# RWKV backward direction reversed in time, its triangles transposed through DRAM, one output accumulator per direction, and preparation handed out by VectorE time

## The chip, the cores and the metric

The kernel runs on one core of a Trainium2 chip, as one launch. The metric is the device time of that launch in microseconds (us). Five engines work beside each other from queues of their own: TensorE (PE in the profile, its weight loads PEld), VectorE (DVE), ScalarE (ACT), GpSimd (POOL) and SyncE (SP), which here issues every DMA. An engine takes its instructions in program order; waits between engines go over semaphores.

## The reference, cut to what matters

One layer of a hybrid block over 512 tokens `x` (width 1024) with 256 context tokens `ctx`: an RWKV-7 mixer, a convolution and an mLSTM side by side, a gated merge, and an MLP, all in float32. The change concerns the RWKV mixer. It has 8 heads of width 64, and its scan is run twice, forward and backward in time, from the state that the same direction left on the context:

```python
def _rwkv7_scan(s0, w, k, v, kk, a, r, reverse, emit):
    ...
    def step(S, inp):
        w_t, k_t, v_t, kk_t, a_t = inp[:5]
        S = (S * w_t[:, :, None, :]
             - jnp.einsum('bhvk,bhk->bhv', S, kk_t)[..., None] * (kk_t * a_t)[:, :, None, :]
             + v_t[..., None] * k_t[:, :, None, :])
        y = jnp.einsum('bhvk,bhk->bhv', S, inp[5]) if emit else None
        return S, y
    S, y = lax.scan(step, s0, xs, reverse=reverse)
    return S, (jnp.moveaxis(y, 0, 1) if emit else None)
...
    for d in range(2):
        rev = d == 1
        s_ctx, yc = _rwkv7_scan(s0, w_c, k_c, fc[2], fc[3], a_c, fc[0], rev, emit_ctx)
        _, yl = _rwkv7_scan(s_ctx, w_l, k_l, fl[2], fl[3], a_l, fl[0], rev, True)
        y_lat = y_lat + yl
```

## The kernel before, in words

Every dense product is three fp32r matmuls over high and low halves of its operands (the weight `raw` is split by ScalarE at L159 and by GpSimd at L160). The 768 tokens are 12 chunks of 64 (`NCH`, `CH`): 0 to 7 are latent, 8 to 11 context. The two directions `d` of a head lie on the two halves of the partitions, `HF[0]` and `HF[1]`. Two heads make a pair `j`, and there are four pairs.

The operands and values of all pairs are made early, in `operands` (a scan over the decays per direction at L386 and L387, products, spills `sp_al` and `sp_bk`) and `values` (`sp_v`). The backward direction has the tokens in the same order as the forward one, so its chunks are visited by the second list of `ORDER`, its masks are upper where the forward ones are lower (`gmf`, `gmb`), and its scan has negative strides.

Class `Rwkv` then has two parts. The **preparation** of a pair (`ctx`, `lat`, `gram`, `transposed`, `invert`) loads the spilled operands, multiplies them chunk by chunk into `pg` (L1006), masks these into `LT`, `LR` and `AL` (L1009, L1011, L1017), and inverts the 64x64 unit triangles in `LT`. For that it cuts each triangle into two 32x32 diagonal blocks, brings them with four VectorE transposes into `N` (L1045; one partition for each of the matrices), runs 30 elimination steps of two instructions each (`tmp` L1050, `N` L1052), transposes the result into `TN` (L1055, L1057) and back into `LT` (L1075, four), and makes the off-diagonal block with small matmuls `px` and `py` (L1066 to L1083). The **chain** runs over the 12 chunks of a pair, one after the other, in three hops a chunk: `ch` (L1133), its negation `xc` on ScalarE (L1137), `ch` (L1139), the copy `UV` (L1142), `ch` (L1148) and the new state `SV` on VectorE (L1149). A chunk of the chain is called a round here; two `SV` instructions, one per direction, end it.

`weave(j)` writes the program of chain `j`: after each of its 36 hops come `PACE[p]` steps of the preparation of pair `j+1` (so many `yield`s of it), then dense matmuls `dg` of the gates and projections (`DENSE`). The output of the pair (`output`, `py`) is accumulated for both directions in one PSUM tile, and `tail(j-1)` normalises it in the next weave. Weave 3 has loads of the modulation weights `wad` in place of a preparation. The preparation of pair 0 runs ahead of the weaves, among the last parts of the mLSTM. The names `x<-y` in the rows are an instruction's written and read tiles.

```python
PACE = [4] * 8 + [3] * 8 + [2] * 12 + [0] * 8
...
            for _ in range(PACE[p] if j < 3 else self.MODS):
                self.paced(last, step(nxt))
```

## Time and profile before

| | |
|---|---|
| three runs | 1365.77, 1371.26, 1374.08 us (median 1371.26) |
| the profiled execution: its time, its span | 1368.34 us, 1366.6 us |
| busy over the span: PE, DVE, ACT, POOL | 1238.3 (91%), 858.2 (63%), 511.2 (37%), 583.0 (43%) us |
| granted TensorE clock, mean | 0.955 of full speed |
| share of the chain of waits: PE, DVE, DMA | 42%, 17%, 6% |
| operands and values | from 131 to 291 us |
| mLSTM fronts and convolution; the mLSTM's end and preparation 0 | 291 to 434; 434 to 531 us |
| weaves 0, 1, 2 | 531 to 793 us |
| weave 3; merge and MLP | 793 to 934; 934 to 1366 us |

The shares are means over stages with different limits. The stages were cut where the first instructions of a part begin; a stage's busy times and its own chain of waits tell what bounds it.

### The profile page before, as it was taken

The numbers are of one execution on the slowest core, as the hardware profiler recorded it, in microseconds if no ns is written. First come the engines' busy times: TensorE is split into PE (matmuls) and PEld (weight loads), VectorE is DVE, ScalarE is ACT, GpSimd is POOL, SyncE is SP. The second block draws the span as 40 slices with busy tenths as digits, with TensorE's granted clock in tenths as the row PEclk, the third lists the DMA queues.
The fourth block names the chain that finished last, engine by engine and source line by source line (L and its number), as shares of the span: only waits on it lengthen the run. The fifth ranks groups of instructions, "written<-read, shape, count | busy, mean of one in ns | idle before, by whom it ended". The sixth has DMA issues, their size and how long they took to land.

```text
span 1366.6 us, 21733 instructions
## 1 busy us (share of the span) xinstructions
PE 1238.3 (91%) x8020; PEld 964.7 (71%) x8020; DVE 858.2 (63%) x1513; ACT 511.2 (37%) x1048; POOL 583.0 (43%) x547
## 2 busy tenths in 40 slices
...
GB/s 375 99 58 63 197 264 245 229 75 70 200 78 91 125 53 150 85 131 60 136 117 48 86 164 146 275 247 234 139 131 142 136 93 93 154 101 95 129 98 87
DMA packets 101457, 187.85 MB, mean 137 GB/s; under 512 B 10708, under 2 KB 29396, under 8 KB 100328
## 3 DMA queue, kind: packets, MB, share of 16 engines
...
HBM read 148.64 MB, written 29.40 MB: 130 GB/s over the span
## 4 chain that ended last, share of the span: by engine, by line
PE 42%; DVE 17%; DMA 6%; issue 2%; ACT 1%; POOL 0%; SPq 0%; DVEq 0%; ACTq 0%; POOLq 0%
PE pt L1301 16%; PE pd L1370 13%; DMA wad<-wada 5%; PE dg L545 4%; DVE N L1052 3%; DVE tmp L1050 3%; PE pg L1006 2%; DVE N L1045 2%; DVE accm L641 1%; PE pd L715 1%; DVE LT L1075 1%; PE ch L1133 1%; DVE SV L1149 1%; PE dl L293 1%; PE ch L1139 1%
## 5 line engine op out<-in xcount | busy, mean ns | idle before, releaser
L160 POOL TENSOR_TENSOR wlo<-raw,whi 128x512 fp32r<-128x512 f32 x296 | 430.8, 1461 | 554.8 <-ACT whi L159 496.3
L159 ACT CAST whi<-raw 128x512 fp32r<-128x512 f32 x296 | 181.7, 619 | 322.0 <-PE pt L1301 114.1
L293 PE MATMUL dl<-hh,whi 128*128 128x512 f32 (+1 forms) x344 | 143.2, 416 | 5.2 <-ACT kT L791 4.3
L293 PE MATMUL dl<-hh,wlo 128*128 128x512 f32 (+1 forms) x344 | 140.5, 408 | 0.0
L293 PE MATMUL dl<-hl,whi 128*128 128x512 f32 (+1 forms) x344 | 139.7, 406 | 0.0
L1370 PE MATMUL pd<-h2h,wlo 128*128 128x512 f32 (+1 forms) x272 | 105.2, 388 | 0.0
L1370 PE MATMUL pd<-h2l,whi 128*128 128x512 f32 (+1 forms) x272 | 104.5, 386 | 0.6 <-POOL h2l L1353 0.6
L1396 DVE TENSOR_TENSOR x<-pt,modb 128x512 f32<-128x512 f32 x8 | 5.5, 691 | 154.8 <-PE pt L1301 154.8
L1370 PE MATMUL pd<-h2h,whi 128*128 128x512 f32 (+1 forms) x272 | 102.3, 383 | 0.2 <-ACT h2h L1350 0.2
L1301 PE MATMUL pt<-whi,h1l 128*128 128x512 f32 x256 | 99.7, 389 | 0.0
L1301 PE MATMUL pt<-whi,h1h 128*128 128x512 f32 x256 | 99.7, 389 | 0.0
L1301 PE MATMUL pt<-wlo,h1h 128*128 128x512 f32 x256 | 99.2, 389 | 0.0
L293 PEld LDWEIGHTS dl<-hh,whi 128*128 128x128 f32 (+1 forms) x344 | 66.9, 194 | 20.4 <-ACT kT L791 4.5
L1374 DVE TENSOR_TENSOR relu<-relu 128x512 f32<-128x512 f32 x32 | 43.7, 1367 | 57.9 <-ACT relu L1373 57.8
L641 DVE SCALAR_TENSOR_TENSOR accm<-wad,scz,accm 128x512 f32<-128x512 f32 x56 | 57.6, 1028 | 34.2 <-DMA wad<-wada 33.6
L293 PEld LDWEIGHTS dl<-hh,wlo 128*128 128x128 f32 (+1 forms) x344 | 66.8, 194 | 14.3 <-issue 0.4
L293 PEld LDWEIGHTS dl<-hl,whi 128*128 128x128 f32 (+1 forms) x344 | 66.6, 194 | 13.8 <-issue 1.3
L1146 POOL TENSOR_TENSOR sps<-SV,PL 64x128 f32<-64x128 f32 x88 | 40.0, 454 | 78.6 <-DVE SV L1149 75.5
L545 PE MATMUL dg<-hl,whi 128*128 128x512 f32 x144 | 65.8, 457 | 0.0
L545 PE MATMUL dg<-hh,whi 128*128 128x512 f32 x144 | 65.0, 451 | 0.0
L545 PE MATMUL dg<-hh,wlo 128*128 128x512 f32 x144 | 64.9, 450 | 0.0
L1370 PEld LDWEIGHTS pd<-h2l,whi 128*128 128x128 f32 x272 | 51.7, 190 | 12.5 <-POOL h2l L1353 0.9
...
## 6 DMA issues: line engine op xcount, KB each, us to landing
...
sp_al<-al SPq DMA_DIRECT2D x8, 640.0 KB, 5.2
```

The lines of the kernel that those rows point to most:

```text
L159: A.copy(hi[:, :], raw[:, :])
L160: G.tensor_tensor(lo[:, :], raw[:, :], hi[:, :], ALU.subtract)
L293: PE.matmul(ps_[0:M, :], lhsT=w[:, ko:ko + M], rhs=x[seg][:, k, :], start=(n == 0), stop=(n == 3 * KT - 1))
L545: yield lambda w=w, x=x, k=k, ko=ko, n=n: PE.matmul(ps[:, :], lhsT=w[:, ko:ko + P], rhs=x[:, k, :], start=(n == 0), stop=(n == 3 * KT - 1))
L641: V.scalar_tensor_tensor(o, t[:, :], sc[:, k, 0:1], o, ALU.mult, ALU.add)
L1006: PE.matmul(ps[hf, i, :, :], lhsT=BK[dd, c, x, :], rhs=al[:, c] if lat else AL[d][dd, 8 + c:9 + c, :], start=True, stop=True)
L1050: V.tensor_tensor(tv, N[:, s + 1:32, s:s + 1].to_broadcast([P, n, s]), N[:, s:s + 1, 0:s].to_broadcast([P, n, s]), ALU.mult)
L1052: V.tensor_tensor(N[:, s + 1:32, 0:s], N[:, s + 1:32, 0:s], tv, ALU.add)
L1146: last["Pool"] = G.tensor_tensor(sps[hf], SV[d][hf, c, :, :], PL[hf, c, :].unsqueeze(2).to_broadcast([64, 2, CH]), ALU.mult)
L1301: PE.matmul(pss[i][:, :], lhsT=x[:, k, ts_], rhs=w[:, :], start=(k == 0 and n == 0), stop=(k == nk - 1 and n == 2))
L1370: PE.matmul(ps[:, ts_], lhsT=w[:, ko:ko + P], rhs=x[:, k, ts_], start=(k == 0 and n == 0), stop=(k == 7 and n == 2))
L1374: V.tensor_tensor(t[:, :], t[:, :], t[:, :], ALU.mult)
```

## The change

The backward half of every operand is turned round in time before it is used: `kr`, `rr` and `vr` are copies by GpSimd with reversed strides, `wdt` and `adt` are written reversed, and the values exist twice in DRAM (`sp_v`, `sp_vr`). Both directions then share one chunk order, one scan of 128 partitions, and masks of one form (`gmo` for a direction's own half of the product, `gmx` for the other). The masks of a chunk group become one instruction of 128 partitions, which writes `LT` and what was `LR`, and two for `AL`.

```diff
-            SY.dma_start(BK[HF[d]], kb[HF[h]])
-            SY.dma_start(rj[HF[d], :], r[HF[h], :])
+            SY.dma_start(BK[HF[d]], kb[d][HF[h]])
+            SY.dma_start(rj[HF[d], :], r[d][HF[h], :])
...
-        V.tensor_tensor_scan(ctf[0:64, :], mkf[0:64], cw[0:64, :], 0.0, ALU.mult, ALU.add)
-        V.tensor_tensor_scan(ctf[64:128, ::-1], mkf[64:128, ::-1], cw[64:128, ::-1], 0.0, ALU.mult, ALU.add)
+        V.tensor_tensor_scan(ctf, mkf, cw[:, :], 0.0, ALU.mult, ALU.add)
...
-        SY.dma_start(sp["bk", hd][:, :], BK.rearrange("p c x t -> p (c x t)"))
+        SY.dma_start(sp["bk", hd][HF[0], :], BK[HF[0]].rearrange("p c x t -> p (c x t)"))
+        for x in range(2):
+            SY.dma_start(sp["bk", hd][HF[1], :].rearrange("p (c x t) -> p c x t", x=2, t=CH)[:, :, 1 - x, :], BK[HF[1], :, x, :])
...
+        vr = S1.tile([P, NCH, 2, CH], F32, tag="kr", name="vr").rearrange("p c x t -> p (c x t)")
+        for a, z in SEG:
+            G.tensor_copy(vr[:, a:z], vj[:, a:z][:, ::-1])
+        for nm, vx in (("v", vj), ("vr", vr)):
+            for c2 in range(2):
+                pt = PS1.tile([P, 3, P], F32, tag="tp", name="tp", bufs=1)
+                for i in range(3):
+                    PE.transpose(pt[:, i, :], vx[:, (c2 * 3 + i) * P:(c2 * 3 + i + 1) * P], ident)
+                vt = S1.tile([P, 3, P], F32, tag="vt", name="vt", bufs=2)
+                A.copy(vt[:, :, :], pt[:, :, :])
+                SY.dma_start(sp[nm, j][c2 * 384:c2 * 384 + 384, :].rearrange("(c t) v -> t c v", t=P), vt[:, :, :])
...
+        kr = S1.tile([P, NCH, 2, CH], F32, tag="kr", name="kr")
+        rr = S1.tile([P, NT], F32, tag="rr", name="rr")
+        for c in (slice(0, 8), slice(8, 12)):
+            G.tensor_copy(kr[:, c], kbs[j][:, c][:, ::-1, :, ::-1])
+        G.tensor_copy(rr[:, :], rj[:, ::-1])
         for h in range(2):
-            operands(j, h, kbs[j], rj)
+            operands(j, h, (kbs[j], kr), (rj, rr))
```

The blocks for the inversion go through DRAM: `LT` is written to `sp_lt` and read back as `N`; after the steps `N` is written to `sp_n` and read back into `LT` in runs of 32 floats. The `TN` transposes become one.

```diff
+        for h, c4 in ((0, 2), (1, 2), (0, 0), (0, 1), (1, 0), (1, 1)):
+            lat = c4 < 2
+            cost = 0.7 if lat else 0.43
+            own = products(h, c4, 0)
+            if masked:
+                other(*masked, 1)
+            yield cost
+            g = h * 12 + c4 * 4
+            dst = LT[:, ::-1, g:g + 4, :] if lat else LT[:, 0:1, g:g + 4, :]
+            V.tensor_tensor(dst.rearrange("p x c t -> p c x t"), own[:, :, :, :], mask("gmo", 2 if lat else 1), ALU.mult)
+            oth = products(h, c4, 1)
+            if c4 == 1:
+                hs = slice(h * 12, h * 12 + 12)
+                SY.dma_start(lt[:, h * 12 * CH:(h + 1) * 12 * CH], LT[:, 0, hs, :].rearrange("p g t -> p (g t)"))
+                for q in range(4):
+                    o, qs = 32 * (q % 2), slice(32 * q, 32 * q + 32)
+                    SY.dma_start(self.N[32 * q + h * 12:32 * q + h * 12 + 12],
+                                 lt[qs, h * 12 * CH:(h + 1) * 12 * CH].rearrange("s (g t) -> g s t", t=CH)[:, :, o:o + 32])
+            yield cost
+            other(h, c4, oth, 0)
+            masked = h, c4, oth
+            yield cost
+        other(*masked, 1)
+        yield cost
...
+        for h in range(2):
+            yield from self.transposed(j, h, (2, 0, 1))
+        if after:
+            after()
+        for s in range(30, 0, -1):
+            n = 31 - s
+            tv = tmp[:, 0:n * s].rearrange("p (t j) -> p t j", t=s)
+            V.tensor_tensor(tv, N[:, 0:s, s:s + 1].to_broadcast([P, s, n]),
+                            N[:, s:s + 1, s + 1:32].to_broadcast([P, s, n]), ALU.mult)
+            V.tensor_tensor(N[:, 0:s, s + 1:32], N[:, 0:s, s + 1:32], tv, ALU.add)
+            yield 0.24 + n * s / 450
+        G.memset(N.rearrange("p a b -> p (a b)")[:, 0:1024:33], 1.0)
+        SY.dma_start(n_[:, :], N.rearrange("p a b -> p (a b)"))
         for q in range(4):
-            d, bl = q // 2, q % 2
-            qs = slice(32 * q, 32 * q + 32)
-            src = LT[qs, :, 32 * bl:32 * bl + 32].rearrange("p g t -> p t g")
-            V.transpose(N[qs] if d == 0 else N[qs].rearrange("p a b -> p b a"), src)
-            yield
-        for s in range(1, 31):
-            n = 31 - s
...
-        G.memset(N.rearrange("p a b -> p (a b)")[:, 0:1024:33], 1.0)
-        V.transpose(TN[0:32].rearrange("p g s -> p s g"), N[0:32].rearrange("p t s -> p s t"))
-        yield
-        V.transpose(TN[96:128].rearrange("p g s -> p s g"), N[96:128])
-        yield
-        xs, ps = [], []
+            o, qs = 32 * (q % 2), slice(32 * q, 32 * q + 32)
+            SY.dma_start(LT[qs, :, o:o + 32], n_[32 * q:32 * q + 24, :].rearrange("g (s t) -> s g t", t=32))
+        V.transpose(TN.rearrange("p g s -> p s g"), N[:, :, :])
...
-        for q in range(4):
-            d, bl = q // 2, q % 2
-            qs = slice(32 * q, 32 * q + 32)
-            src = N[qs] if d == 0 else N[qs].rearrange("p a b -> p b a")
-            V.transpose(LT[qs, :, 32 * bl:32 * bl + 32].rearrange("p g t -> p t g"), src)
```

The chain's `UU` copies go, since `UV` now keeps each direction on its own half; the output gets one PSUM tile per direction, which the tail adds; each step of the preparation yields its VectorE time, and a hop takes steps until 1.3 us are given out; loads are moved.

```diff
-PACE = [4] * 8 + [3] * 8 + [2] * 12 + [0] * 8
+PACE = 1.3
...
+            for d, nm in enumerate(("v", "vr")):
+                src = self.sp[nm, j][c4 * 4 * CH:(c4 + 1) * 4 * CH, :].rearrange("(c t) v -> t c v", t=CH)
+                for dst in (SV[d], UV[d]):
+                    SY.dma_start(dst[HF[1 - d], cs].rearrange("p c h v -> p c (h v)"), src)
...
-        py = self.py = self.PSC.tile([P, NT], F32, tag="o", name="py")
...
+        py = self.py = [self.PSC.tile([P, NT], F32, tag=("o", "ob")[d], name="py") for d in range(2)]
...
-                o = py[HF[h], c * CH:(c + 1) * CH]
                 for d in range(2):
-                    PE.matmul(o, lhsT=self.SV[d][:, c, h, :], rhs=self.AL[d][sl[h]][:, c, :], start=(d == 0), stop=False)
-                PE.matmul(o, lhsT=self.UU[:, c, h, :], rhs=self.LR[sl[h]][:, c, :], start=False, stop=True)
+                    o = py[d][HF[h], c * CH:(c + 1) * CH]
+                    PE.matmul(o, lhsT=SV[d][:, c, h, :], rhs=self.AL[d][sl[h]][:, c, :], start=True, stop=False)
+                    PE.matmul(o, lhsT=UV[d][HF[d], c, h, :], rhs=LR[HF[d], h * 12 + c, :], start=False, stop=True)
...
-            for d, c, ch, hf in zip(range(2), cs, chs, HF):
-                if c < 8:
-                    last["ACT"] = A.copy(self.UU[hf, c, :, :], ch[HF[0], 1])
...
+        def spend():
+            nonlocal budget, over
+            c = next(nxt, None)
+            over = c is None
+            budget -= c or 0
...
-            for _ in range(PACE[p] if j < 3 else self.MODS):
+            if j < 3:
+                budget += PACE
+                while budget > 0 and not over:
+                    self.paced(last, spend)
...
+            if p == 30 and j < 3:
+                self.load(j + 1, (0,))
...
-            self.load(j + 1, (0, 1))
+            self.load(j + 1, (1,))
+        if j < 2:
+            self.fetch(j + 2, "lat")
...
-        A.copy(y[:, :], self.py[:, :])
+        A.copy(y[:, :], self.py[0][:, :])
+        V.tensor_tensor(y[:, :], y[:, :], self.py[1][:, ::-1], ALU.add)
```

Three places of the program's order. On VectorE, the second round of weave 1: from one pair of `SV` to the next, before (its first two rows, then the masks of half a chunk group each; the next `SV` stand behind the cut):

```order
L1149 TENSOR_TENSOR SV_4802<-ch_5941,sps_6005 64x128
L1149 TENSOR_TENSOR SV_4803<-ch_5942,sps_6011 64x128
L1009 TENSOR_TENSOR LT_3243<-pg,cst 64x256
L1011 TENSOR_TENSOR LR_3250<-pg,cst 64x256
L1017 TENSOR_TENSOR AL_3249<-pg,cst 64x4x2x64
L1227 SCALAR_TENSOR_TENSOR y<-pm,y 128x512
L1009 TENSOR_TENSOR LT_3243<-pg,cst 64x256
L1011 TENSOR_TENSOR LR_3247<-pg,cst 64x256
L1017 TENSOR_TENSOR AL_3245<-pg,cst 64x4x2x64
L1009 TENSOR_TENSOR LT_3243<-pg,cst 64x256
L1011 TENSOR_TENSOR LR_3250<-pg,cst 64x256
L1017 TENSOR_TENSOR AL_3249<-pg,cst 64x4x2x64
```

and after:

```order
L1178 TENSOR_TENSOR SV_4881<-ch_5957,sps_6010 64x128
L1178 TENSOR_TENSOR SV_4882<-ch_5958,sps_6016 64x128
L1268 SCALAR_TENSOR_TENSOR y<-pm,y 128x512
L1035 TENSOR_TENSOR LT_3336<-pg,cst 128x4x2x64
L1024 TENSOR_TENSOR AL_3337<-pg,cst 64x4x2x64
L1024 TENSOR_TENSOR AL_3338<-pg,cst 64x4x2x64
L1035 TENSOR_TENSOR LT_3336<-pg,cst 128x4x2x64
L1024 TENSOR_TENSOR AL_3339<-pg,cst 64x4x2x64
L1024 TENSOR_TENSOR AL_3340<-pg,cst 64x4x2x64
L1178 TENSOR_TENSOR SV_4881<-ch_6047,sps_6095 64x128
L1178 TENSOR_TENSOR SV_4882<-ch_6048,sps_6101 64x128
```

The same masks come as sets of one 128-partition and two 64-partition instructions, and two sets stand between the pairs of `SV`; the `N` transposes that followed these rows before have no place in the new order.

On VectorE, the end of the inversion in weave 1, before:

```order
L1050 TENSOR_TENSOR tmp<-N 128x30
L1052 TENSOR_TENSOR N<-N,tmp 128x30
L1149 TENSOR_TENSOR SV_4802<-ch_6690,sps_6716 64x128
L1055 STREAM_TRANSPOSE TN<-N 32x32x32
L1149 TENSOR_TENSOR SV_4803<-ch_6691,sps_6722 64x128
L1057 STREAM_TRANSPOSE TN<-N 32x32x32
L1075 STREAM_TRANSPOSE LT_3243<-N 32x32x32 x4
L1009 TENSOR_TENSOR LT_4789<-pg,cst 64x256
```

and after:

```order
L1082 TENSOR_TENSOR tmp<-N 128x30
L1084 TENSOR_TENSOR N<-N,tmp 128x30
L1178 TENSOR_TENSOR SV_4881<-ch_6656,sps_6713 64x128
L1178 TENSOR_TENSOR SV_4882<-ch_6657,sps_6719 64x128
L1091 STREAM_TRANSPOSE TN<-N 128x32x32
L1035 TENSOR_TENSOR LT_4872<-pg,cst 128x256
L1024 TENSOR_TENSOR AL_4873<-pg,cst 64x256
L1024 TENSOR_TENSOR AL_4874<-pg,cst 64x256
```

One transpose of 128 partitions stands where six of 32 stood; the masks that follow are the next pair's.

On SP, where that inversion ends, before (values and operands of the next pair, then weights):

```order
L1100 DMA SV_4802<-sp_v_113 64x4x128
L1100 DMA SV_4803<-sp_v_113 64x4x128
L1100 DMA SV_4802<-sp_v_113 64x4x128
L1100 DMA SV_4803<-sp_v_113 64x4x128
L974 DMA AL_4791<-sp_al_119 64x1024
L974 DMA AL_4792<-sp_al_119 64x1024
L974 DMA AL_4794<-sp_al_121 64x1024
L974 DMA AL_4795<-sp_al_121 64x1024
L156 DMA raw<-wblk 128x512
L550 DMA sp_g_139<-gt 128x512
L156 DMA raw<-wblk 128x512 x2
```

and after:

```order
L159 DMA raw<-wblk 128x512
L1087 DMA sp_n_122<-N 128x1024
L1130 DMA UV_4879<-sp_v_119 64x4x128
L1130 DMA UV_4880<-sp_vr_120 64x4x128
L1090 DMA LT_3336<-sp_n_122 32x24x32 x4
L984 DMA AL_4873<-sp_al_128 64x1024
L569 DMA sp_g_150<-gt 128x512
L1130 DMA SV_4881<-sp_v_119 64x4x128
L1130 DMA SV_4882<-sp_vr_120 64x4x128
L984 DMA AL_4874<-sp_al_128 64x1024
L984 DMA AL_4875<-sp_al_130 64x1024
L984 DMA AL_4876<-sp_al_130 64x1024
```

The write of `N` and the four reads into `LT` now stand among these loads, and the loads behind the reads are issued after them.

## Rows read from the trace of the kernel before

**Rows 1.** Busy time by engine in five stretches, with granted clock and DMA:

```profile
core 0: us, PE busy (x) PEld busy (x) DVE busy (x) ACT busy (x) POOL busy (x), PEclk, DMA share, GB/s
...
131.00:291.00 160.00, 141.61 (x659) 108.86 (x658) 130.43 (x144) 92.61 (x144) 63.18 (x49) 0.95 0.71 215
...
434.00:531.00 97.00, 77.66 (x577) 64.78 (x576) 79.20 (x210) 22.54 (x42) 37.42 (x40) 0.91 0.30 95
...
619.00:708.00 89.00, 81.25 (x975) 57.65 (x972) 71.99 (x141) 34.02 (x98) 29.64 (x42) 0.92 0.30 90
...
708.00:793.00 85.00, 76.92 (x889) 53.81 (x888) 70.23 (x136) 32.89 (x96) 31.42 (x41) 0.98 0.28 87
...
793.00:934.00 141.00, 121.79 (x756) 86.21 (x755) 97.66 (x170) 50.73 (x122) 63.32 (x57) 0.94 0.68 215
```

**Rows 2.** Chain of waits, shares by line, for 434 to 531 and 619 to 708:

```profile
by line: DVE tmp L1050 12.7%; DVE N L1052 12.3%; PE dl L293 10.7%; DVE LT L1075 8.8%; DVE N L1045 8.7%; issue 3.9%; DMA gbc<-sp_rows 3.5%; DMA SV<-sp_v 2.9%; DVE rsq L73 2.6%; PE pt L889 2.5%; DVE gbc L859 2.3%; DVE rsqt L71 2.3%; DVE TN L1
...
by line: PE dg L545 14.6%; DVE N L1052 13.2%; PE pg L1006 11.2%; DVE tmp L1050 10.0%; issue 6.6%; DVE N L1045 6.1%; PE ch L1139 3.3%; DVE SV L1149 3.3%; DVE AL L1017 3.3%; PE pbk L1031 3.1%; PE ch L1133 3.1%; DVE LT L1009 2.4%; DVE TN L1055
```

**Rows 3.** Timeline of VectorE in weave 1 (start, length, instruction):

```profile
624.60 0.61 DVE L1149 TENSOR_TENSOR SV<-ch,sps 64x128 f32<-64x128 f32 x2 [0.74 <-PE ch L1148]
...
637.08 0.61 DVE L1149 TENSOR_TENSOR SV<-ch,sps 64x128 f32<-64x128 f32 x2
...
643.03 4.29 DVE L1045 STREAM_TRANSPOSE N<-LT 32x1024 f32<-32x1024 f32 x2
...
655.42 0.61 DVE L1149 TENSOR_TENSOR SV<-ch,sps 64x128 f32<-64x128 f32 x2
...
694.88 0.29 DVE L1149 TENSOR_TENSOR SV<-ch,sps 64x128 f32<-64x128 f32 x1
...
697.22 8.41 DVE L1075 STREAM_TRANSPOSE LT<-N 32x1024 f32<-32x1024 f32 x4
...
714.64 0.60 DVE L1149 TENSOR_TENSOR SV<-ch,sps 64x128 f32<-64x128 f32 x2
```

**Rows 4.** Groups by line: busy us, mean ns of one, idle before:

```profile
L1050 DVE TENSOR_TENSOR tmp<-N 128x30 f32<-128x30 f32 (+14 forms) x120 | 52.6, 438 | 3.1
...
L1052 DVE TENSOR_TENSOR N<-N,tmp 128x30 f32<-128x30 f32 (+14 forms) x120 | 54.9, 458 | 3.0
...
L1045 DVE STREAM_TRANSPOSE N<-LT 32x1024 f32<-32x1024 f32 x16 | 33.0, 2059 | 0.2
...
L1075 DVE STREAM_TRANSPOSE LT<-N 32x1024 f32<-32x1024 f32 x16 | 33.4, 2089 | 0.4
...
L1055 DVE STREAM_TRANSPOSE TN<-N 32x1024 f32<-32x1024 f32 x4 | 8.4, 2090 | 0.1
...
L1009 DVE TENSOR_TENSOR LT<-pg,cst 64x256 f32<-64x256 f32 x48 | 20.2, 421 | 47.8 <-PE pg L1006 46.7 <-PE ch L1139 0.6
...
L1011 DVE TENSOR_TENSOR LR<-pg,cst 64x256 f32<-64x256 f32 x32 | 13.2, 414 | 0.0
...
L1017 DVE TENSOR_TENSOR AL<-pg,cst 64x512 f32<-64x512 f32 (+1 forms) x48 | 28.8, 600 | 0.7
...
L386 DVE TENSOR_TENSOR_SCAN ct<-scm,cw 64x768 f32<-64x768 bf16 x8 | 17.7, 2213 | 0.3
```

**Rows 5.** Two steps of the inversion, GpSimd beside the first; a GpSimd group:

```profile
670.01 1.36 DVE L1050 TENSOR_TENSOR tmp<-N 128x228 f32<-128x228 f32 x1
...
671.84 0.41 DVE L1050 TENSOR_TENSOR tmp<-N 128x234 f32<-128x234 f32 x1
...
669.82 1.31 POOL L1250 TENSOR_TENSOR y<-y,bo 128x512 f32<-128x512 f32 x1
...
L811 POOL TENSOR_SCALAR to<-to 128x512 f32<-128x512 f32 x4 | 6.1, 1532 | 0.0
```

**Rows 6.** DMA issues: size of each and median us to landing:

```profile
sp_al<-al SPq DMA_DIRECT2D x8, 640.0 KB, 5.2
...
SV<-sp_v SPq DMA_DIRECT2D x24, 128.0 KB, 2.9
```

More of the change, by code (lines that the diff above doesn't have):

```diff
@@ L135, in build @@
             sp["bk", 2 * j + h] = DR.tile([P, 2 * T], F32, name=f"sp_bk{j}{h}")
-        sp["v", j] = DR.tile([T, P], F32, name=f"sp_v{j}")
+        for nm in ("v", "vr"):
+            sp[nm, j] = DR.tile([T, P], F32, name=f"sp_{nm}{j}")
+        sp["lt", j] = DR.tile([P, 24 * CH], F32, name=f"sp_lt{j}")
+        sp["n", j] = DR.tile([P, 1024], F32, name=f"sp_n{j}")
     for g in range(24):
@@ L394, in operands @@
         E3 = E.rearrange("p (c t) -> p c t", t=CH)
[L395 to L396 removed]
+        G.tensor_copy(PL[:, j, :, h:h + 1], E3[:, :, CH - 1:CH])
         al = SO.tile([P, 20 * CH], F32, tag="al", name="al", bufs=2)
@@ L514, in build @@
     rw.open_a()
-    rw.run(rw.ctx(0), rw.lat(0))
+    rw.fetch(0, "ctx")
+    rw.fetch(0, "lat")
+    rw.run(rw.prepare(0))
     st[2] = front(2)
@@ new lines, in grams, with products @@
+        lt = self.sp["lt", j]
+        masked = None
+        def products(h, c4, x):
+            AL, BKt, BK = self.head(j, h)
+            lat = c4 < 2
+            pool, tag = ((self.PS, "g"), self.PG)[x]
+            ps = pool.tile([P, 4, 2 if lat else 1, CH], F32, tag=tag, name="pg")
+            for i in range(4):
+                c = c4 * 4 + i
+                for d in range(2):
+                    dd, hf = HF[d], HF[(d + x) % 2]
+                    al = AL[d][dd, 0:16, :].rearrange("p (x c) t -> p c x t", x=2)[:, c] if lat else AL[d][dd, 8 + c:9 + c, :]
+                    PE.matmul(ps[hf, i, :, :], lhsT=BK[dd, c, (d + x) % 2, :], rhs=al, start=True, stop=True)
+            return ps
```

212 lines of the change are left out of this document (85 added, 127 removed).

## The prediction, made before the changed kernel was run

> **What bounds the kernel now.** I read the stages first [rows 1]: five stretches in which the change does anything, each with the busy time of its engines. In the operands and values (131 to 291 us) VectorE is busy for 130.43 of 160 us and TensorE for 141.61. Where the mLSTM ends and preparation 0 is inverted (434 to 531) VectorE has 79.20 of 97 and TensorE 77.66. In weaves 1 and 2 TensorE has 81.25 of 89 and 76.92 of 85, VectorE 71.99 and 70.23. So two engines are nearly full and neither is full, which is the picture of a chain that hands over between them. The merge and the MLP from 934 us on are TensorE's alone and aren't touched.
>
> Then the chain of waits of two of these stretches [rows 2]. In 434 to 531 the reader should add up VectorE's inversion: `tmp` 12.7%, `N` 12.3%, and the transposes `LT` 8.8% and `N` 8.7%. In weave 1 the first is a dense product (14.6%), then `N` 13.2%, `pg` 11.2%, `tmp` 10.0% and the `N` transposes 6.1%. Preparation is thus on the path in both places, in weave 1 together with TensorE.
>
> Last the timeline of VectorE in weave 1 [rows 3]: the `SV` pairs are the clock of the chain. The first round ends with the pair at 637.08, the second with one that is not shown, the third with the pair at 655.42; the three take 655.42 − 624.60 = 30.8 us. From the last `SV` of the weave to the first of the next, 694.88 to 714.64, lie 19.8 us, with four `LT` transposes of 8.41 us in them.
>
> **What VectorE is spared.** Per preparation [rows 4]: four `N` transposes by 2.059 us are 8.2; four `LT` by 2.089 are 8.4; two `TN` become one, 2.1. The masks were 12 of 0.421, 8 more of about that for `LR`, and 12 of 0.600, 15.6 us together. After it is six sets of one wide instruction (0.6 for a 512-element one, 0.42 for a 256) and two 64-partition ones of the same lengths: 4 x 1.8 + 2 x 1.26, some 10 us. I take 11, so −4.7. The 30 steps (0.438 and 0.458) stay as many and as large. Together −23 of VectorE's work in each of four preparations. What of it is time is a matter of each stage.
>
> **Weaves 0 to 2.** In the first three rounds of weave 1, 8.2 of the 30.8 us are `N` transposes, two of them in the one row of 4.29 us and two more like them behind it [rows 3]. They go; the masks and their `pg` stay, at (30.8 − 8.2)/3 = 7.5 us a round, and the order shows two sets between `SV` pairs. The chain of waits credits these transposes with only 6.1% of 89, 5.4 us [rows 2], so the gain lies between 5.4 and 8.2; I take 7.5, since nothing but masks stands beside them in the order. At the boundary the 8.4 us of `LT` transposes go. In their place comes a trip through DRAM, which the order starts on SP before the weave's last rounds. I take −5 of 8.4, because the chunk's values and operands are loaded there as well and the next chain still has to wait for the `px` and `py`. Against this, the second output accumulator adds 32 matmuls a weave. TensorE's mean record in weave 1 is 81.25/975 = 0.083 us [rows 1], so between 0 and 2.7; I take 2. The tail's additional VectorE instruction is 0.7, by the wide mask rows. ScalarE loses eight `UU` copies, which I price at 0: the hop's next matmul waits for the other copy. Sum −7.5 − 5 + 2 + 0.7 = −9.8 a weave, taken as −10, with −6 and −14 as its ends. The steps of the inversion are as many in a round as before, so I expect nothing from the new `PACE` there.
>
> **434 to 531.** The transposes hold 17.5% of 97 us, 17.0, of the chain of waits [rows 2]. TensorE's 77.66 busy us stand close behind VectorE's 79.20, so not all of it comes out. The DRAM trips are under the mLSTM's own work. I take −12, with −4 and −18 as the ends.
>
> **Operands and values.** Eight of the sixteen scans go, by 2.213 us [rows 4]: −17.7 on an engine that is busy 130 of 160. Against that stand the reversed copies: per pair 1536 elements for `kr`, 512 for `rr`, 768 for `vr`. The nearest GpSimd row has 512 elements in 1.532 us, 3.0 ns an element [rows 4, 5], so 2816 x 3.0 = 8.4 us a pair and 34 in all, on an engine busy 63.18 of 160 [rows 1]. `operands` waits for them ahead of each backward load. A copy beside VectorE can also cost VectorE: a step of 234 elements alone took 0.41 us, one of 228 beside a GpSimd product 1.36 [rows 5]. If each of the copies met one such instruction fully, 16 copies would cost 16 x 0.95 = 15. Twenty-four more transposes and eight more evictions for `vr` go to TensorE and ScalarE, which have room. I take −2, with −12 (most of the scans' time comes out) and +15 as ends.
>
> The GPSIMD Engine Reference of the Trainium skill (Specifications) says that GpSimd shares its SBUF interfaces with VectorE and contends with VectorE instructions that have two SBUF inputs. The pair 1.36 and 0.41 us agrees with that; the sum above already carries the row.
>
> **The rest.** Weave 3 loses its `LT`-and-`N` boundary with weave 2 (counted) and gains a tail instruction: +1. SP: the write to `sp_n`, its reads and the writes to `sp_lt` stand ahead of operand and weight loads, and SP waits there for VectorE and for landings. A weave's weights are few and prefetched; at 0, and if the cover is gone this is the fourth rival's price.
>
> **Sum**: 3 x −10 − 12 − 2 + 1 = −43. The profiled execution took 1368.3 us, 0.2% below the median of 1371.3, which I leave as it is: 1368.3 − 43 = **1325**.
>
> **The rivals.**
> *TensorE takes the place of the transposes.* For it: 81.25 of 89 busy, and a dense product heads the chain of weave 1 [rows 1, 2]. Then a weave can give back only its idle 7.8 us less the 2 for more matmuls, and of this perhaps two thirds: −4. The stage before gives −6, the front nothing: −18, **1350**. Against it: TensorE's ends are modelled, so waits are in the busy figure.
> *The front eats it.* The copies of 34 us lie on the path ahead of each pair's operands, the 15 of contention come to them, and a third of the scans' 18 comes out: 34 + 15 − 6 = +43. With the −41 of the other stages that is +2, **1370**. For it: this stage has 141.61 of 160 on TensorE and both engines wait for operands. Against it: GpSimd has 97 free us there.
> *The DRAM trips are slow, and the kernel with them.* A preparation has two trips: 1536 runs of 128 bytes twice over into `N`, 3072 such runs back into `LT`. The nearest rows [rows 6]: 640 KB land in 5.2 us, so 512 KB written and again read in 4.2 each, 8.4 a trip at the least; 256 runs of 512 bytes land in 2.9 us, and if runs were to land one group after another, 3072 would take 12 x 2.9 = 35. About 9 us are covered, by the six `transposed` steps of the first trip and by the last rounds of the second. I take 9 to 12, nearer to the low end, since the DMA share of these stages is 0.28 to 0.30 [rows 1] and the rows' 2.9 us are mostly a fixed part. Each weave would change by −10 + 2 x (trip − 9); it decides from a trip of 14 us. At 18 us a weave is 8 longer, 434 to 531 gives nothing, and the end is 1368 + 24 − 2 + 1 = **1391**.
>
> The Trainium skill speaks for this last rival: DMA: Bandwidth & Descriptors (Specifications) wants 512 bytes in a transfer for line rate, and names a read-modify-write below; VectorE: DVE Perf Modes (The three transpose paths) calls VectorE's transpose the fastest for 32x32 and a copy with transposing strides 19 times slower than the transposing DMA. No run here has such a DMA. By the row of VectorE four 32x32 sets take 8.4 us, and by the bounds above a trip takes 8.4 to 39: no rule settles it, because the trip isn't on VectorE.
>
> *The change doesn't do what it says* has no room of its own: the order shows the transposes gone.
>
> **Chances.** Forecast 0.52 (all its ends together are 1297 and 1362; 1300 to 1345 holds most of it), TensorE 0.24 (1340 to 1358), the front 0.13 (1357 to 1380), slow trips 0.11 (from 1380). A measurement of this kernel tells about 1% from no change, 13.7 us. Faster by over 1% (below 1357.6): 0.52 and nearly all of 0.24, so 0.75; within it 0.14; slower 0.11. For 8 in 10 the range leaves out the slow trips and the far half of the front: 1295 to 1366.
>
> **What would show it.** In the profile after: no VectorE transposes but one `TN` of some 2 us a preparation; the first three intervals of `SV` in weave 1 at 7 to 8 us each in place of 30.8 together; the boundary at 14 to 16; `LT<-sp_n` landing within 12 us; 434 to 531 shorter by a tenth; the front of the same length, with GpSimd busier by about 34. I'm wrong if TensorE is over 95% busy in weaves that are as long as before, if the first `ch` of a weave waits for `sp_n`, or if `BK<-kr` waits for GpSimd on the path.

## The result, and the profile after

The changed kernel took 1424.68 us (median of four runs, 1409.76 to 1432.52) against 1370.16 us: 1.0363 times as long, interval 1.0274 to 1.0451. It is slower, where I forecast 1325. Ratios here and below are of undisturbed executions alone, which leaves out the one at 1432.52. The profiled execution took 1409.76 us with a span of 1408.0, 41.4 over that of before; it is the fastest of the four, and the mean clock that it was granted, 0.943, the highest (0.925, 0.930 and 0.933 in the others; before 0.955).

The 41.4 us lie between these events of the two traces:

| from, to | before | after | change |
|---|---|---|---|
| start to the first `pg` of preparation 0 | 362.7 | 384.0 | +21.3 |
| to the start of the mLSTM's last `yc` | 164.5 | 160.2 | −4.3 |
| to the end of the first `SV` pair of weave 0 | 10.2 | 19.8 | +9.6 |
| weave 0, between first `SV` pairs | 87.8 | 87.7 | −0.1 |
| weave 1 | 90.0 | 99.6 | +9.6 |
| weave 2 | 87.9 | 90.0 | +2.1 |
| weave 3, to the first `pd` of the merge | 122.5 | 126.9 | +4.4 |
| from there to the end | 441.0 | 439.8 | −1.2 |

The windows of the changed kernel, first the operands, then 434 to 531, the three weaves, and a stretch of weave 1 (columns as in [rows 1]):

```profile
core 0: us, PE busy (x) PEld busy (x) DVE busy (x) ACT busy (x) POOL busy (x), PEclk, DMA share, GB/s
131.00:291.00 160.00, 128.55 (x559) 96.12 (x558) 116.04 (x136) 79.58 (x128) 72.77 (x59) 0.88 0.75 207
434.00:531.00 97.00, 90.01 (x663) 78.08 (x663) 56.45 (x192) 27.75 (x53) 41.99 (x45) 0.95 0.33 104
564.00:651.70 87.70, 85.56 (x914) 59.88 (x911) 41.64 (x102) 29.23 (x78) 28.49 (x41) 0.98 0.45 123
651.70:751.30 99.60, 97.46 (x956) 68.06 (x955) 47.67 (x119) 30.45 (x80) 31.38 (x44) 0.86 0.40 115
751.30:841.30 90.00, 88.27 (x925) 61.70 (x923) 45.14 (x115) 30.57 (x80) 31.11 (x42) 0.98 0.37 106
700.00:730.00 30.00, 30.00 (x161) 19.54 (x160) 9.66 (x31) 4.74 (x14) 4.93 (x9) 0.56 0.15 47
```

VectorE is relieved as meant: 56.45 us busy from 434 to 531 where it had 79.20 [rows 1], 41.64 to 47.67 in a weave where it had 70 to 72. TensorE is not. It fills the weaves to 98%, and in 700 to 730 it is busy for the whole 30 us at a granted clock of 0.56.

Weave 1 in the chain of waits, which answers to the second line of [rows 2]:

```profile
by line: PE dg L564 32.3%; PE py L1146 10.0%; PE py L1145 9.9%; PE pg L1011 8.1%; PE ch L1162 4.7%; DVE tmp L1082 4.3%; PE ch L1168 4.0%; PE ch L1177 3.8%; DMA N<-sp_lt 3.7%; DVE N L1084 2.9%; DMA sp_lt<-LT 2.5%; issue 1.4%; SPq L1043 1.2%;
```

The transposes are gone from it, and the output's `py`, which had no place among the named lines before, holds 10.0 + 9.9%.

The sign that I had named for being wrong has come: TensorE over 95% busy in weaves as long as before.

VectorE's timeline of weave 1 answers to [rows 3]:

```profile
651.14 0.60 DVE L1178 TENSOR_TENSOR SV<-ch,sps 64x128 f32<-64x128 f32 x2 [1.28 <-POOL wlo L163]
...
658.88 0.60 DVE L1178 TENSOR_TENSOR SV<-ch,sps 64x128 f32<-64x128 f32 x2
...
667.90 0.60 DVE L1178 TENSOR_TENSOR SV<-ch,sps 64x128 f32<-64x128 f32 x2
...
673.76 0.29 DVE L1178 TENSOR_TENSOR SV<-ch,sps 64x128 f32<-64x128 f32 x1 [0.68 <-PE ch L1177]
...
728.99 0.61 DVE L1178 TENSOR_TENSOR SV<-ch,sps 64x128 f32<-64x128 f32 x2 [6.34 <-PE ch L1177]
729.62 1.95 DVE L1091 STREAM_TRANSPOSE TN<-N 128x1024 f32<-128x1024 f32 x1
...
750.68 0.61 DVE L1178 TENSOR_TENSOR SV<-ch,sps 64x128 f32<-64x128 f32 x2 [0.16 <-POOL wlo L163]
```

From the end of one `SV` pair to the next, the first three intervals are 22.3 us in place of 30.8, at 7.7, 9.0 and 5.6 a round, and one `TN` of 1.95 us is the only transpose. The last `SV` of the weave, though, comes at 729, and from there to the next weave's first it takes 21.7 us in place of 19.8. The last three intervals before it, during which the output is accumulated, take 9.2, 12.5 and 10.5 us; before they took 4.3, 5.2 and 7.1.

TensorE in one of those output steps of weave 2 (each float32 matmul leaves two records):

```profile
804.00 0.33 PE L1145 MATMUL py<-AL,SV 128*64 128x64 f32 x2
804.26 0.33 PE L1146 MATMUL py<-LT,UV 64*64 64x64 f32 x2
804.52 0.33 PE L1145 MATMUL py<-AL,SV 128*64 128x64 f32 x2
804.77 0.32 PE L1146 MATMUL py<-LT,UV 64*64 64x64 f32 x2
```

A matmul of 128 rows alternates with one of 64, and each takes 0.257 us to the start of the next. With 64 of them a weave that is 16.4 us. The groups of the output matmuls in this kernel:

```profile
L1145 PE MATMUL py<-AL,SV 128*64 128x64 f32 x256 | 44.6, 260 | 0.0
L1146 PE MATMUL py<-LT,UV 64*64 64x64 f32 x256 | 44.4, 258 | 0.0
```

### The profile page after: what moved, and what is told of

Same layout as the page of the kernel before. It is cut to its first block, busy times and chain, and to the rows that moved or that the text cites. A ratio compares the mean times of both kernels' runs of the same rounds, so it can differ in the third digit from the quotient of the medians.

```text
span 1408.0 us, 22052 instructions
## 1 busy us (share of the span) xinstructions
PE 1294.6 (92%) x8172; PEld 999.5 (71%) x8172; DVE 751.2 (53%) x1419; ACT 497.8 (35%) x986; POOL 576.4 (41%) x555
## 4 chain that ended last, share of the span: by engine, by line
PE 59%; DMA 7%; DVE 6%; issue 1%; SPq 1%; ACT 1%; POOL 0%; DVEq 0%; ACTq 0%; POOLq 0%
PE pt L1342 15%; PE pd L1411 13%; PE dg L564 7%; PE dl L296 5%; PE pg L1011 3%; PE py L1146 2%; PE py L1145 2%; DMA wad<-wada 2%; DVE tmp L1082 2%; PE ch L1162 1%; DVE N L1084 1%; PE dp L643 1%; PE ch L1168 1%; DMA N<-sp_lt 1%; PE ch L1177 1%
## 5 line engine op out<-in xcount | busy, mean ns | idle before, releaser
L163 POOL TENSOR_TENSOR wlo<-raw,whi 128x512 fp32r<-128x512 f32 x296 | 401.2, 1360 | 537.3 <-ACT whi L162 473.1
L1342 PE MATMUL pt<-whi,h1l 128*128 128x512 f32 x256 | 99.6, 389 | 0.0
L1342 PE MATMUL pt<-whi,h1h 128*128 128x512 f32 x256 | 99.6, 389 | 0.0
L1166 ACT ACTIVATE xc<-ch 64x128 f32<-64x128 f32 x96 | 26.0, 271 | 137.6 <-PE ch L1162 136.2
L1415 DVE TENSOR_TENSOR relu<-relu 128x512 f32<-128x512 f32 x32 | 39.3, 1230 | 61.3 <-ACT relu L1414 61.2
L1178 DVE TENSOR_TENSOR SV<-ch,sps 64x128 f32<-64x128 f32 x88 | 25.3, 287 | 75.8 <-PE ch L1177 65.6
```

The costliest lines, as they stand in the source:

```text
L163: G.tensor_tensor(lo[:, :], raw[:, :], hi[:, :], ALU.subtract)
L1342: PE.matmul(pss[i][:, :], lhsT=x[:, k, ts_], rhs=w[:, :], start=(k == 0 and n == 0), stop=(k == nk - 1 and n == 2))
L1415: V.tensor_tensor(t[:, :], t[:, :], t[:, :], ALU.mult)
```

## The experiments

Each kernel was timed beside the kernel before on the same chip, and several sets were run; between sets the ratios compare. The theory: a matmul whose number of rows differs from that of the one ahead of it has to wait for that one, and the new output order makes every output matmul such a one. A second loss sits in the front, a third ahead of weave 0. Rivals: two accumulators in two banks, or the greater count, slow `py`; GpSimd's reversed copies slow the front; the DRAM trips slow the weaves.

**Output by shape.** Four matmuls of 128 rows, then four of 64, per chunk, in the changed kernel:

```diff
-            for h in range(2):
-                for d in range(2):
-                    o = py[d][HF[h], c * CH:(c + 1) * CH]
-                    PE.matmul(o, lhsT=SV[d][:, c, h, :], rhs=self.AL[d][sl[h]][:, c, :], start=True, stop=False)
-                    PE.matmul(o, lhsT=UV[d][HF[d], c, h, :], rhs=LR[HF[d], h * 12 + c, :], start=False, stop=True)
+            o = {(d, h): py[d][HF[h], c * CH:(c + 1) * CH] for d in range(2) for h in range(2)}
+            for d in range(2):
+                for h in range(2):
+                    PE.matmul(o[d, h], lhsT=SV[d][:, c, h, :], rhs=self.AL[d][sl[h]][:, c, :], start=True, stop=False)
+            for d in range(2):
+                for h in range(2):
+                    PE.matmul(o[d, h], lhsT=UV[d][HF[d], c, h, :], rhs=LR[HF[d], h * 12 + c, :], start=False, stop=True)
```

> The changed kernel with the output's matmuls of a chunk written by shape: first the four of 128 rows, then the four of 64, in place of alternating. Theory (a change of the number of rows between one matmul and the next empties TensorE, 0.15 us each time, so the 64 output matmuls of a weave take 64 x 0.257 = 16.4 us in place of 48 that took 4.0): a step of eight falls from 2.06 to about 0.8 us, py from 16.4 to 6 to 7 us a weave, four weaves -40, so 1425 - 40 = 1385 and a ratio to the kernel before of 1.01. Rival (two accumulators in two PSUM banks, or simply 16 more matmuls, cost the time): the banks and the count stay, so 1420 to 1425, ratio 1.036.

Measured: 1369.52 us, ratio to before 1.0012 (0.9984 to 1.0041). TensorE's timeline of that kernel shows two steps in weave 0, each eight records of either shape:

```profile
614.27 0.45 PE L1145 MATMUL py<-AL,SV 128*64 128x64 f32 x8
614.65 0.34 PE L1148 MATMUL py<-LT,UV 64*64 64x64 f32 x8
614.93 0.45 PE L1145 MATMUL py<-AL,SV 128*64 128x64 f32 x6
```

The first eight matmuls take 0.66 us from 614.27 to 614.93, where eight took 2.06. The shape theory holds; banks and count are the same. The gain is 48 us by the two ratios (55 by the medians), where 40 were expected. Added up over the trace, the time from the start of each output matmul to TensorE's next matmul is 70.3 us in the changed kernel and 21.7 us here; the spans of the two profiled executions differ by 37.4 (1408.0 and 1370.6). In weave 1 the stretch at 0.56 has no counterpart here (the weave's clock is 0.93 over 84.9 us).

**All output matmuls over 128 rows.**

```diff
-                    PE.matmul(o, lhsT=UV[d][HF[d], c, h, :], rhs=LR[HF[d], h * 12 + c, :], start=False, stop=True)
+                    PE.matmul(o, lhsT=UV[d][:, c, h, :], rhs=LR[:, h * 12 + c, :], start=False, stop=True)
```

> The changed kernel with the second matmul of each output pair over all 128 rows, so that all output matmuls have one shape; it adds the other half's products into the output, which is thereby not the reference's. Order, count and banks stay. Shape theory: py falls from 0.257 us to about 0.06 to 0.12 each, 4 to 8 us a weave, some -40 in all, 1370 to 1390 in this one look. Rival (banks or count): py stays at 0.25, 1410 to 1430.

One run alone: 1367.95 us. Its output groups:

```profile
L1145 PE MATMUL py<-AL,SV 128*64 128x64 f32 x256 | 27.3, 238 | 0.0
...
L1146 PE MATMUL py<-LT,UV 128*64 128x64 f32 x256 | 26.1, 228 | 0.0
```

Order, banks and count are those of the changed kernel, and the loss is gone. The groups' means, 238 and 228 ns, are hardly below 260 and 258 there: the mean length of a record does not show the wait, the distance of starts does: the sum that was 70.3 us is 27.2 here.

**The same change of shape, put into the kernel before.**

```diff
-                PE.matmul(o, lhsT=self.UU[:, c, h, :], rhs=self.LR[sl[h]][:, c, :], start=False, stop=True)
+                PE.matmul(o, lhsT=self.UU[HF[0], c, h, :], rhs=self.LR[sl[h]][HF[0], c, :], start=False, stop=True)
```

> The kernel before with the third output matmul of each chunk and head over 64 rows in place of 128; it leaves out the backward direction's own-chunk part of the output. Count, bank and accumulators stay as before, only the shape now changes four times a chunk, 32 times a weave. Shape theory, at 0.15 to 0.2 us a change by the changed kernel's trace: +5 to 6 us a weave, +15 to 25 in all, 1383 to 1393. Rival (the changed kernel's loss came from the two accumulators): no change, 1368 within 4.

Measured: 1389.11 us, ratio 1.0157 (1.0124 to 1.0189), +21.5 us, with one accumulator and the old count:

```profile
L1114 PE MATMUL py<-AL,SV 128*64 128x64 f32 x256 | 29.2, 238 | 0.0
...
L1115 PE MATMUL py<-LR,UU 64*64 64x64 f32 x128 | 21.2, 247 | 0.0
```

Divided by 4 x 32 changes of shape this is 0.17 us each. The sum of distances goes from 21.7 us in the kernel before to 40.8. The cause of the output's loss is shown from both sides.

**A buffer of its own for `vr`.** In the changed kernel's trace GpSimd's first reversed copy of values is late:

```profile
248.89 3.17 POOL L455 COPY vr<-vj 128x512 f32<-128x512 f32 x2 [0.68 <-DMA BK<-kr]
```

It waits for a load from `kr`, the last one, since `vr` has `kr`'s single buffer. The values of all pairs follow behind it. The first and the last `bo`, VectorE's product in `values`, start there at the times below; before they started at 225.5 and 263.6 us.

```profile
256.46 0.69 DVE L467 TENSOR_TENSOR bo<-hs,vj 128x512 f32<-128x512 f32 x1 [1.54 <-PE hs L465]
...
302.71 0.69 DVE L467 TENSOR_TENSOR bo<-hs,vj 128x512 f32<-128x512 f32 x1
```

```diff
-        vr = S1.tile([P, NCH, 2, CH], F32, tag="kr", name="vr").rearrange("p c x t -> p (c x t)")
+        vr = S1.tile([P, T], F32, name="vr")
```

> The changed kernel with a tile of its own for vr, which shared the single buffer of kr. Theory (values 0 waits with its vr copy until the last load from kr has landed, 249 us, so all values follow the operands): the last bo falls from 303 to 265 to 275 us, the first SV of weave 0 from 564 to 528 to 540, time -25 to -35, 1390 to 1400, ratio 1.015. Rival (GpSimd's reversed copies and their contention with VectorE cost the time): the copies stay, so the last bo stays near 300 and the time within 5 us of 1425.

Measured: 1406.2 us (four runs, 1395.62 to 1420.39), ratio 1.0248 (1.0158 to 1.0339), some 16 us less than the changed kernel by the ratios, whose intervals overlap. The mechanism holds, the size not: the first `bo` comes at 233.2 us but the last at 286.9, and the first `SV` pair ends at 547.0, 17 us earlier. The profiled execution, 1415.67 us, doesn't show this as time: its weaves 0 to 2 took 91.4, 105.4 and 99.2 us at clocks of 0.93, 0.81 and 0.86, against 0.98, 0.86 and 0.98 in the changed kernel.

**Both.**

> Both edits, output matmuls by shape and a tile of its own for vr. If the two losses are independent, -40 and -30: 1350 to 1358, ratio 0.985 to 0.99. If one hides the other (weave 0 waits for the mLSTM's end anyway), 1375 to 1385. If the slow-down is elsewhere, 1420.

Measured: 1360.76 us, ratio 0.9941 (0.9911 to 0.997). Beside the output by shape alone the buffer is worth 9 us, and the two intervals don't meet. This version beats both kernels, by 0.6% the one before.

**Without any reversed values, and with values reversed on TensorE.** The first loads `sp_v` for both directions and drops `vr`. The second makes the reversed rows from the transposed ones:

```diff
+    J = S1.tile([P, P], F32, name="J")
+    G.tensor_copy(J[:, :], ident[:, ::-1])
...
+            pr = PS1.tile([P, 3, P], F32, tag="tp", name="tpr", bufs=1)
+            PE.matmul(pr[:, :, :], lhsT=J[:, :], rhs=vt[:, :, :], start=True, stop=True)
+            vr = S1.tile([P, 3, P], F32, tag="vt", name="vtr", bufs=4)
+            A.copy(vr[:, :, :], pr[:, ::-1, :])
```

> The kernel with the output by shape and without any vr: no reversed copy of the values, 24 transposes and 8 evictions fewer, and the backward direction is loaded with the forward values, so that its output is not the reference's. It prices what the reversed values still cost beside the shared buffer. If they are what is left in the front (last bo at 291 us with the own buffer, 264 before the change): bo at 262 to 268, time -14 to -20 against 1360.8, 1341 to 1347. Rival (the reversed kr and rr and the port of GpSimd are what is left): within 5 of 1361.

> The kernel with the output by shape, the reversed values made from the transposed ones by one matmul with a reversed unit matrix (no GpSimd copy, no second transpose) and four vt buffers in place of two. If the front's remaining loss is GpSimd's copy and the buffers behind it: bo at 270 to 278, 1345 to 1353. If it is the chain through the one PSUM buffer (four evictions a pair in place of two), bo stays at 288 to 292 and the time within 5 of 1361.

Measured: 1349.2 us, ratio 0.9863 (0.9834 to 0.9893), without reversed values; the last `bo` is at 263.0 us, as before the change and as expected; the gain of 11 us is less than the 14 to 20 that were. The first `pg` comes at 361.2, before at 362.7: up to there the reversed values are all that the front lost, and `kr` and `rr` come out even with the scans that they spare. Reversed by a matmul: 1352.16 us, ratio 0.9896 (0.9863 to 0.9929), the best complete version. Its last `bo` is still late:

```profile
237.25 0.67 DVE L472 TENSOR_TENSOR bo<-hs,vj 128x512 f32<-128x512 f32 x1
...
290.70 0.69 DVE L472 TENSOR_TENSOR bo<-hs,vj 128x512 f32<-128x512 f32 x1
```

That speaks for the chain through one PSUM buffer as to `bo`, against it as to the time, which is 8.6 us less (6 by the ratios, whose intervals overlap): neither of the two expectations is met as a whole.

**The first DRAM trip undone**, in the version with both repairs:

```diff
-                SY.dma_start(lt[:, h * 12 * CH:(h + 1) * 12 * CH], LT[:, 0, hs, :].rearrange("p g t -> p (g t)"))
...
+        flat = self.LT[j % 2].rearrange("p x g t -> p (x g) t")
+        for q in range(4):
+            o, qs = 32 * (q % 2), slice(32 * q, 32 * q + 32)
+            V.transpose(N[qs].rearrange("p s t -> p t s"), flat[qs, 0:32, o:o + 32].rearrange("p g t -> p t g"))
+            yield 2.1
...
-PACE = 1.3
+PACE = 1.55
```

> The kernel with both repairs (1360.8), with the first DRAM trip undone: N is again filled by four VectorE transposes of 2.06 us, 8.2 us a preparation, with the budget a hop raised from 1.3 to 1.55 us so that the preparation ends at the same hop. My prediction's step (the N transposes are on the path in the weaves and in the mLSTM's end) wants +5 to +8 a weave and +5 before them: 1380 to 1390. Rival (TensorE has become the bound, 73.6 of 76.8 us busy in weave 0, VectorE has 43 to 49 of 77 to 87, and covers the transposes): within 5 of 1361.

Measured: 1369.61 us, ratio 0.9999 (0.9965 to 1.0033), 8.9 us over the 1360.76 (8 by the ratios, whose intervals just meet): as a total between the two expectations. By stage the two profiled executions tell more:

| | both repairs | `N` by transposes again | change |
|---|---|---|---|
| first `pg` to the end of the last `yc` | 162.1 | 154.9 | −7.2 |
| weaves 0, 1, 2 together | 246.0 | 266.4 | +20.4 |
| weave 3 | 120.1 | 114.8 | −5.3 |

In the weaves twelve transposes, some 25 us of VectorE, cost 20 us, which is the +5 to +8 a weave of my step; the clock there is lower too (0.92, 0.90 and 0.87, against 1.00, 0.92 and 0.93), and TensorE's longer busy time is 6.8 of the 20. The chain of weave 0 names the transposes again:

```profile
by line: PE dg L564 34.8%; PE pg L1011 11.0%; DVE N L1074 7.3%; PE ch L1167 6.5%; PE ch L1161 6.2%; PE ch L1176 5.8%; SPq L1087 5.3%; DMA raw<-wblk 4.6%; DMA sp_n<-N 4.3%; PE py L1142 3.7%; PE pbk L1055 2.8%; PE py L1145 2.6%; SPq L569 1.9%
```

Ahead of the weaves the same four transposes cost nothing: that stage is shorter without the trip.

**The reads of both trips issued twice**, in the version with the flip matmul:

```diff
-                    SY.dma_start(self.N[32 * q + h * 12:32 * q + h * 12 + 12],
+                    for _ in range(2):
+                        SY.dma_start(self.N[32 * q + h * 12:32 * q + h * 12 + 12],
...
-            SY.dma_start(LT[qs, :, o:o + 32], n_[
+            for _ in range(2):
+                SY.dma_start(LT[qs, :, o:o + 32], n_[
```

> The kernel with the output by shape and the values reversed by a matmul (1352.2), with every read of the two DRAM trips issued twice: 32 more reads into N and 16 more into LT, 24,576 more runs of 128 bytes. If the trips are covered by other work, as the six us of DMA on the chain of weave 1 in the changed kernel suggest: within 5 of 1352. If small runs are the price that my fourth rival named (trips on the path, at 4 to 5 us a read group): +4 to +5 a trip, eight trips, 1385 to 1390.

Measured: 1399.49 us, ratio 1.0201 (1.0131 to 1.0272), +47 by the medians and +42 by the ratios: more than either expectation. The waits of weaves 0 to 2 (in total, times, longest), with reads once and twice:

```profile
DVE tmp L1087 <- DMA N<-sp_lt: 4.5, 2, 3.3
```

```profile
DVE tmp L1088 <- DMA N<-sp_lt: 34.1, 3, 14.7
```

With reads once a trip into `N` ends just in time: 4.5 us of waiting in all, and one wait of `tmp` of 3.1 us more that the profile puts down to another load. Behind `tmp` on VectorE stand the `SV` of the chain, so a trip that is too long stops the chain. In weave 1 one round took 22.1 us in place of 7.4. A second read into the same place also waits for the first to land, and SP, which issues them, stood still 26.7 us for this in the three weaves; so the run prices a trip of twice the length and later loads behind it, and not more traffic alone.

**Values ahead of the next pair's operands.** The changed kernel loads pair 1's operands ahead of pair 0's values, and the first matmul of the chain waits for those:

```profile
545.33 5.09 SPq L984 DMA_DIRECT2D AL<-sp_al  x8
550.47 0.62 SPq L1130 DMA_DIRECT2D SV<-sp_v  x1
```

```profile
555.84 0.66 PE L1162 MATMUL ch<-SV,AL 128*64 128x64 f32 x4 [11.77 <-DMA SV<-sp_v]
```

Before, that wait was 4.21 us.

```diff
+    rw.load(0, (2, 0, 1))
     rw.fetch(1, "ctx")
     rw.fetch(1, "lat")
-    rw.load(0, (2, 0, 1))
```

> The kernel with the output by shape and the values reversed by a matmul (1352.2), with the values of pair 0 loaded ahead of the operands of pair 1 instead of behind them. Theory: the first matmul of the first chain waits 11.5 us for SV, because SP issues 2.5 MB of operands ahead of it; that wait falls to 2 to 4 us, the first SV comes 7 to 9 us earlier, time 1343 to 1346. Rival: the masks of weave 0 then wait for the operands, the wait moves into pg, and the time stays within 4 of 1352.

> The changed kernel with that order of loads alone, both other losses left in. If the three losses are independent: -7 to -9 against the changed kernel's 1425, 1416 to 1418. If the front's delay hides it (the first chain is late anyway), within 3 of 1425.

Measured: 1364.66 us, ratio 0.9948 (0.9918 to 0.9978), which is no gain over the 0.9896 (0.9863 to 0.9929) of the version with the other order; and 1420.26 us, ratio 1.0356 (1.031 to 1.0401), in the changed kernel, 4 less with an interval that holds no change. The wait itself did shrink:

```profile
537.10 0.66 PE L1169 MATMUL ch<-SV,AL 128*64 128x64 f32 x4 [4.16 <-DMA SV<-sp_v]
```

But the weave that follows took 92.6 us in place of 77.2. The windows of the two kernels, from the wait on, first with operands ahead and then with values ahead:

```profile
core 0: us, PE busy (x) PEld busy (x) DVE busy (x) ACT busy (x) POOL busy (x), PEclk, DMA share, GB/s
...
536.00:548.00 12.00, 7.79 (x90) 6.17 (x91) 1.92 (x6) 1.07 (x4) 0.82 (x4) 0.56 0.90 163
548.00:580.00 32.00, 31.28 (x319) 22.25 (x320) 17.18 (x42) 11.06 (x30) 13.87 (x19) 1.00 0.47 121
```

```profile
536.00:544.50 8.50, 7.04 (x34) 4.85 (x35) 0.58 (x2) 1.33 (x5) 0.79 (x3) 0.50 0.63 187
544.50:597.00 52.50, 48.61 (x418) 33.94 (x416) 19.89 (x49) 13.08 (x35) 16.62 (x23) 0.81 0.45 112
```

With the long wait (11.50 us here) the weave ran at 1.00 of the clock; without it its first 52.5 us ran at 0.81. At the chain's start both stretches stand near half speed (0.56 and 0.50), and the kernel that waited reached full speed at its end. The masks did not wait for the operands there, but `tmp` waited 6.9 us once, where it had waited 3.3. So 8 us of waiting went, and the weave behind it took 15 more. TensorE's busy time in the weave rose by 13.5 us (73.7 to 87.2) and its idle time by 1.9, and 52.5 us at 0.81 are by estimate 10 us longer than at 1.00. The changed kernel shows the same with that order: weave 0 took 106.0 us at 0.83, in place of 87.7 at 0.98. That the clock is what gave the gain back was thus seen in two pairs of traces and not tried by itself.

**A larger budget a hop.**

```diff
-PACE = 1.3
+PACE = 2.0
```

> The kernel of the run beside it (values first) with a budget of 2.0 us of VectorE a hop in place of 1.3, so that a preparation ends after two thirds of the weave. If TensorE's work bounds the weaves, where the steps stand is the same: within 5 of the run beside it. If the handing-out by VectorE time matters (masks and steps ahead of the SV they delay), rounds 1 to 6 grow by 1.5 to 2 us each and the last ones shrink less: +5 to +12.

Measured: 1357.68 us, ratio 0.991 (0.9873 to 0.9947), against 0.9948 (0.9918 to 0.9978) beside it: the intervals overlap. The 5 to 12 us more that were expected if the handing-out matters did not come; where the steps stand within a weave is worth less than this can tell.

## Why the prediction was wrong

**The step that failed** is "the second output accumulator adds 32 matmuls a weave … between 0 and 2.7; I take 2". I priced the new matmuls (16 a weave, which leave 32 records) by the mean record of the weave and the old ones at no change. In the changed order each of the 64 takes 0.257 us, 16.4 a weave; sorted by shape it is 0.66/8 = 0.083, 5.3 a weave. From start to start the output of one weave takes 16.1 to 19.6 us in the trace, where the 48 matmuls of before took 4.6 to 4.9 in weaves 0 to 2: the term of 2 measured 11 to 15. Grouping them by shape gave some 50 us back. The edit is two lines of the diff that I read for what they compute and not for the order of their shapes. A chain of waits in which `py` isn't named can't warn of it; the kernel before had the wide shape throughout in its output. The Trainium skill, TensorEngine Tiling (Array Packing), Tiling Modes, lists 128×64 and 64×64 as different modes and says "Mode switching requires drain". The runs agree as far as the cost goes, with 0.17 us a change put into the kernel before and 0.257 us from start to start in the changed one; that the array empties is not to be seen in them. I didn't weigh that page.

**The weaves.** The first three intervals of `SV` came as I wrote in their sum, 8.5 us less, and not one by one (7.7, 9.0 and 5.6, where I wanted 7 to 8 each). The boundary did not: 21.7 us, where I wanted 14 to 16. Its chain of waits, before (695 to 716 us) and after (729 to 752), is

```profile
by line: PE dg L545 50.2%; PE pg L1006 9.4%; PE ch L1139 7.1%; PE px L1081 6.3%; PE py L1114 5.9%; PE ch L1133 5.3%; PE px L1066 4.9%; PE px L1067 4.9%; PE py L1115 2.4%; PE ch L1148 1.8%; PE px L1082 1.5%; PE pbk L1031 1.2%
```

```profile
by line: PE dg L564 47.2%; PE py L1145 9.0%; PE py L1146 8.8%; PE ch L1162 5.0%; PE pg L1011 4.6%; PE px L1101 4.5%; PE px L1110 4.2%; PE px L1111 3.9%; PE px L1100 3.4%; PE ch L1168 3.2%; PE ch L1177 3.2%; ACT gt L568 2.6%; ACT UV L1171 0.
```

Dense products fill it in both kernels, so the `LT` transposes stood beside TensorE's work there and not ahead of it. With the output mended and the flip matmul the three weaves take 77.2, 85.2 and 78.9 us, 24.4 less than before, −8.1 a weave against my −10. There the spared VectorE time was path, as undoing the first trip shows too (+20 in the weaves).

**434 to 531.** I took −12; from the first `pg` to the last `yc` it was −4.3. In the changed kernel the chain of this stretch (434 to 544 us), and two of its pieces in order of time, read

```profile
by line: PE dl L296 41.0%; DVE tmp L1082 8.7%; DVE N L1084 7.6%; DMA LT<-sp_n 5.4%; PE st L859 3.1%; PE acc L894 2.9%; PE acc L893 2.8%; DMA gbc<-sp_rows 2.8%; DMA sp_n<-N 2.6%; PE px L1111 2.1%; DVE gbc L880 2.0%; issue 1.9%; PE psc L871 1
...
463.40 2.86 DMA sp_n<-N
...
467.77 5.89 DMA LT<-sp_n
```

TensorE's `dl` has taken the place of the transposes, which was the mechanism of my rival on TensorE. And the second trip, which I had put under the mLSTM's work, is on the path, with 10.3 us from 463.40 to its landing at 473.66, though TensorE itself stood idle for it for 2.0 us only. Undoing the first trip, with its transposes back, made the stage 7.2 us shorter.

**The front.** I took −2 and it was +21 up to the first `pg`. My rival on the front named the right stage and the wrong mechanism: not the time of the copies (0.96 to 3.66 us for the `vr` copies of a pair) nor contention with them, but one buffer that `vr` shares with `kr`, and the longer way of the values. With no reversed values the front is as before.

**SP.** "At 0" was wrong by 9.6 us ahead of weave 0, where 5.09 us of operand issues and their landing stand ahead of the first values. Mending it gave nothing back as a whole, by the traces because of the clock in the weave behind it.

**The slow trips**, my rival for a slower kernel, were not the cause in the weaves: VectorE waited 7.8 us for `N` in the three weaves of the changed kernel. They were close to it, as the doubled reads show.

Without the output's loss and with the values reversed by the matmul the kernel is 18.5 us shorter than before in the traces, where I forecast 43: up to the first `pg` +8.1, to the last `yc` −7.0, to the first `SV` pair +9.4, the three weaves −24.4, weave 3 −4.2, the rest −0.3. So the relief in the weaves was near to what I wrote, and the other terms were not. I took the VectorE time that is spared for path in every stage, in a kernel whose TensorE was busy for 91% of the span, and looked for the cost of the change only on the engines it was made for.
